# A hybrid decoder layer on one core: the opening loads cut smaller and put on two queues, with small matmuls of ones between the first products

## The chip, the cores and the metric

The kernel runs on one core of a Trainium2 chip. The metric is the device time of one execution in microseconds; where several runs were timed, the median is given. The profile is one execution taken by the hardware profiler, and its times are counted from the start of its span.

## What is computed

One layer of a decoder step, for 1,024 prompt tokens and 8 x 4 sample tokens, at a model width of 1,024, all in float32. Cut to its frame:

```python
h = rms(x, n_mix_pre)
z = h @ w_in                       # q | k | v | u, 512 + 128 + 128 + 512 columns
a = sliding_window_attention(q, k, v, sinks)
m = pool_mixer(u) @ w_pool * pool_scale
x = x + rms(concat(a, m) @ w_out, n_mix_post)
f = rms(x, n_ffn_pre)
x = x + rms((silu(f @ w_gate) * (f @ w_up)) @ w_down, n_ffn_post)
x = x + sigmoid(x @ w_ple_gate) * (p @ w_ple)
```

The change concerns the first product alone, the `u` columns of `h @ w_in`, and the loads and casts ahead of it.

## The kernel before

The 1,056 tokens are cut into three groups `g` of 352. Activations lie with their features on the 128 partitions and their tokens along the free axis, so x of one group is eight tiles of 128 x 352, held as two halves `h` of four tiles each. The text calls half `h` of group `g` x(g,h). A weight of 1,024 x 128 is eight tiles of 128 x 128, again used in two halves.

To keep float32 accuracy with float32r operands, each operand is split in two: a part `hi` (weights `wh`) that ScalarE casts to float32r, and the remainder `lo` (weights `wl`) that VectorE subtracts (`split`, L163). A product is then three matmuls per tile: `wh` with `hi`, `wh` with `lo`, `wl` with `hi`. For x the cast also multiplies by the norm's gain `gn` (`x_operand`, L359: ScalarE at L364, VectorE at L366). The norm's own factor per token is applied only afterwards, at the eviction of `u` (L476).

The opening goes like this. Constants and a table of ones are made on GpSimd; the gains are loaded over ScalarE's queue (L139, called at L142). ScalarE computes a square root once, so that its table is loaded (L343). TensorE runs 8 matmuls of ones with ones, of 128 columns in float32 (L346). SP issues all the other loads in a fixed order (`load`, L339; L392 to L402): the first half of weight 0, x(0,0) in two parts, the first halves of weights 1 to 3, x(0,1), the second halves of weights 0 and 1, x(1,0), the second halves of weights 2 and 3, x(1,1). The casts on ScalarE and the subtractions on VectorE are pinned to the order in which they are written, from L403 to L415 (`fixed`): the first half of weight 0, x(0,0), the first halves of weights 1 to 3, x(0,1), the second halves of weights 0 and 1, x(1,0), the second halves of weights 2 and 3, and then the squares of x(0,0) and x(0,1) on ScalarE (L375) and their sum over the eight tiles on VectorE (`sum_halves`, L326), which gives `acc`. What comes after on these two engines is not pinned: the tool that builds the program places it by a schedule of its own.

TensorE's matmuls are pinned throughout (`pinned`, L485). The order is: for each half, the products of weights 0 to 3 with group 0 (`u_prod`, L461: per tile `wh` with `hi` and `wh` with `lo`, then four times `wl` with `hi`); then the norm of group 0, in two steps of `rstd_steps` (L292). The first step sums `acc` over the partitions (L300), ScalarE takes the root (L302), VectorE the reciprocal (L303) and builds two diagonal matrices `dg` (L310). Between the steps TensorE does the product of weight 0 with x(1,0). The second step multiplies `dg` by ones (L320), which spreads the factor over the partitions. Then the products with groups 1 and 2, the other columns of `w_in`, attention, the output projection and the feed-forward, which fills most of the span.

Of the kernel before, what the change touches and what calls it, by code (L numbers as in the profile page):

```python
# [11 lines left out]
F32R = mybir.dt.float32r  # L12
AF = mybir.ActivationFunctionType
# [3 lines left out]
P = 128  # L17
D = 1024
KC = D // P
# [35 lines left out]
WARM = 8  # L55
# [6 lines left out]
def trunk_kernel(  # L62
# [31 lines left out]
    nc = tc.nc  # L94
    te, ve, se, ge = nc.tensor, nc.vector, nc.scalar, nc.gpsimd
# [10 lines left out]
    def nm(s):  # L106
        cnt[0] += 1
        return f"{s}{cnt[0]}"

    def act_tile(shape, dt=F32, s="a"):  # L110
        return apool.tile(shape, dt, tag="a", bufs=A_SLOTS, name=nm(s))

    def half(g, dt=F32, s="h"):
        return act_tile([P, 4, NS[g]], dt, s)
# [9 lines left out]
    def mm(*args, **kw):  # L124

        ins = te.matmul(*args, **kw)  # L126
        if pinned[0]:
            tc.keep_in_program_order(ins)

    def bank():  # L130
        return psum.tile([P, 512], F32, tag="b", name=nm("b"))
# [4 lines left out]
    def const(shape, src=None, s="c", dt=F32):  # L136
        t = cpool.tile(shape, dt, name=nm(s))
        if src is not None:
            nc.scalar.dma_start(t, src)  # L139
        return t  # L140

    gn = const([P, 4, KC], gains)  # L142
    psc, skp, skd = const([P, 4]), const([P, 8]), const([P, 2])
    ident = const([P, P])
    make_identity(nc, ident)
    ones = const([P, P])
# [3 lines left out]
    epst = const([P, 1])  # L150
# [3 lines left out]
    plan = []  # L154
# [3 lines left out]
    def fix(ins):  # L158

        if fixed[0]:  # L160
            tc.keep_in_program_order(ins)

    def split(hi, lo, src):  # L163
        fix(se.copy(hi, src))  # L164
        fix(ve.tensor_tensor(lo, src, hi.bitcast(F32), op=ALU.subtract))  # L165

    raws, pairs = {}, {}
# [9 lines left out]
    def w_tile(shape, s):  # L177
        return wpool.tile(shape, F32R, tag="wp", bufs=2 * W_PAIRS, name=nm(s))
# [45 lines left out]
    for s, gs in WALK:  # L224
        pairs_of = []
        for i in range(SLAB):
            c = SLAB * s + i
# [108 lines left out]
        return r.unsqueeze(1).to_broadcast([P, 4, r.shape[1]])  # L336


    def load(dst, src):  # L339
        tc.keep_in_program_order(nc.sync.dma_start(dst, src))  # L340


    tc.keep_in_program_order(se.activation(const([P, 1]), epst, AF.Sqrt))  # L343
    warm = bank()
    for _ in range(WARM):
        te.matmul(warm[:, :P], ones, ones, start=True, stop=True)  # L346

    xr = {}

    def x_load(g, h, n=1):  # L350
        xr[g, h] = half(g, s="xr")
        for c in range(0, 4, 4 // n):
            cs = slice(c, c + 4 // n)
            k = slice(4 * h + c, 4 * h + c + 4 // n)
            load(xr[g, h][:, cs, :], x[:, k, OFF[g] : OFF[g + 1]])

    xs, acc1, r1 = [[None] * 2 for _ in range(G)], [None] * G, [None] * G

    def x_operand(g, h):  # L359
        t = xr[g, h]  # L360
        hi, lo = half(g, F32R), half(g, F32R)
        for c in range(4):
            gc = gn[:, 0, 4 * h + c : 4 * h + c + 1]
            fix(se.activation(hi[:, c, :], t[:, c, :], AF.Identity, scale=gc))  # L364
            fix(
                ve.scalar_tensor_tensor(  # L366
                    lo[:, c, :], t[:, c, :], gc, hi[:, c, :].bitcast(F32), op0=ALU.mult, op1=ALU.subtract
                )
            )
        xs[g][h] = hi, lo  # L370

    def x_squares(g):
        sqs = [xr[g, h] for h in range(2)]
# [2 lines left out]
        acc1[g] = sum_halves(sqs, g)  # L376


    def u_load(c, h):
        j = U0[c]  # L380
        if h == 0:
            shape = plan[j][1]
            raws[j] = act_tile(shape) if c == 3 else wpool.tile(shape, F32, tag="wr", bufs=W_RAW, name=nm("wr"))
        load(raws[j][:, 4 * h : 4 * h + 4, :], plan[j][0][:, 4 * h : 4 * h + 4, :])

    def u_split(c, h):
        j = U0[c]
        if h == 0:
            pairs[j] = w_tile(plan[j][1], "wh"), w_tile(plan[j][1], "wl")
        split(*(t[:, 4 * h : 4 * h + 4, :] for t in pairs[j]), raws[j][:, 4 * h : 4 * h + 4, :])  # L390

    u_load(0, 0)  # L392
    x_load(0, 0, 2)
    for c in range(1, 4):
        u_load(c, 0)
    x_load(0, 1)
    for c in range(2):
        u_load(c, 1)
    x_load(1, 0)
    for c in range(2, 4):  # L400
        u_load(c, 1)
    x_load(1, 1)  # L402
    fixed[0] = True  # L403
    u_split(0, 0)
    x_operand(0, 0)
    for c in range(1, 4):
        u_split(c, 0)
    x_operand(0, 1)
    for c in range(2):
        u_split(c, 1)  # L410
    x_load(2, 0)
    x_operand(1, 0)
    for c in range(2, 4):
        u_split(c, 1)
# [4 lines left out]
    for dst, src in ((psc, pscale), (skp, sink_p), (skd, sink_d)):  # L419
        load(dst, src)  # L420
# [12 lines left out]
    n = 4 * NDEC * PST  # L433
# [27 lines left out]
    def u_prod(c, g, h):  # L461

        if h == 0:
            ups[c, g] = bank()
        ps = ups[c, g][:, : NS[g]]
        wh, wl = pairs[U0[c]]
        xh, xl = xs[g][h]
        for k in range(4):
            mm(ps, wh[:, 4 * h + k, :], xh[:, k, :], start=h == 0 and k == 0, stop=False)
            mm(ps, wh[:, 4 * h + k, :], xl[:, k, :], start=False, stop=False)  # L470
        for k in range(4):
            mm(ps, wl[:, 4 * h + k, :], xh[:, k, :], start=False, stop=h == 1 and k == 3)

# [14 lines left out]
    for h in range(2):  # L488
        for c in range(4):
            u_prod(c, 0, h)  # L490
    u_norm(norms[0], 0)
    u_prod(0, 1, 0)
    x_operand(2, 0)
    u_norm(norms[0], 0)
    x_squares(1)
    for c in range(4):
        u_evict(c, 0)
        if c:
            u_prod(c, 1, 0)
# [79 lines left out]
    for c in range(4):  # L579
        n = NDEC * DSEQ  # L580
# [67 lines left out]
    def scores(b):  # L648


        t = act_tile([P, 8, WIN])
        cur = [bank() for _ in range(2)]
        prv = [bank() for _ in range(2)] if b else None
        for c in range(4):
            for which, at in ((cur, b), (prv, b - 1)):
                if which is None:
                    continue
                for kv in range(2):
                    rows = slice(64 * kv, 64 * kv + 64)
                    mm(  # L660
                        which[kv][:, c * WIN : (c + 1) * WIN],
                        qT[c][rows, b * WIN : (b + 1) * WIN],
                        kT[rows, at * WIN : (at + 1) * WIN],
                        start=True,
                        stop=True,
                    )
        for kv in range(2):
            tk = t[:, 4 * kv : 4 * kv + 4, :]
            if b:
                se.copy(tk, v4(prv[kv]))  # L670
                ve.copy_predicated(tk, m4(0).bitcast(mybir.dt.int32), v4(cur[kv]))  # L671
            else:
                ve.tensor_tensor(tk, v4(cur[kv]), m4(1), op=ALU.add)
            hs = slice(4 * kv, 4 * kv + 4)
            softmax(tk, 4, 0.125, skp[:, hs], nskp[:, hs])
        return t
# [145 lines left out]
    t = scores(order[0])  # L822
# [15 lines left out]
    for a, b in zip(order, order[1:] + [None]):  # L838
# [5 lines left out]
        t = t2  # L844
# [421 lines left out]
```

## Time and profile before

| | us |
|---|---|
| median of 3 runs | 1123.25 |
| lowest and highest | 1122.29, 1125.07 |
| the profiled execution | 1121.84 |
| its span | 1120.1 |
| TensorE busy in the span | 1108.9 |
| VectorE busy | 748.4 |
| ScalarE busy | 440.7 |

In the rows below, a row of the timeline has the start, the busy time, the engine, the line, the operation with its output and inputs, a count, and in brackets the idle time of that engine before it and what ended it. PE is TensorE, DVE is VectorE, ACT is ScalarE, SPq is SyncE's queue of load instructions. A row of waits has the engine and line, what it waited for, and the total, the number of times and the longest in us. A row of stretches has the stretch, its length, the busy time of PE, weight loads, DVE, ACT and POOL with their counts, then TensorE's granted clock as a share of full, the share of the DMA engines and GB/s. A row of load issues ends in the KB of one load and the us from its issue to its landing.

### The profile page before, as it was taken

The page shows a single profiled execution, that of the slowest core. Times are in us where ns is not written, and L with a number is a line of the kernel's source. Part 1 is how long each engine was busy: PE and PEld are TensorE (multiplying, and loading weights), DVE is VectorE, ACT ScalarE, POOL GpSimd, SP SyncE. Part 2 cuts the span into 40 slices and gives each one's busy share as a digit, 9 for nine tenths or more (in the row PEclk, how much of TensorE's full clock was granted, in tenths as well). Part 3 has the DMA queues.
Part 4 walks back from the last instruction along what each step waited for, and adds up shares of the span by engine and source line. Part 5 has one row for each costly group of instructions (what it writes and reads, how often), then busy time and mean ns, then how long its engine had stood idle before and what let it go on. Part 6 is the DMA issues. An engine that isn't in the chain of part 4 may idle for free.

```text
span 1120.1 us, 17702 instructions
## 1 busy us (share of the span) xinstructions
PE 1108.9 (99%) x7171; PEld 1090.8 (97%) x7171; DVE 748.4 (67%) x1244; ACT 440.7 (39%) x782; POOL 179.5 (16%) x152
## 2 busy tenths in 40 slices
PE   8999999999999999999999999999999999999998
PEld 8999988899999999999999999999999999999998
DVE  6667468985879955355554555557887877789532
ACT  8323276664646524331321314124424334366220
POOL 0045132200000041011111101111132123100000
PEclk9999999999999999999999999999999999999999
DMA  8121311272543312111110212112212222246211
GB/s 288 57 70 43 119 41 38 83 265 71 206 159 132 114 38 76 39 61 54 38 57 20 75 38 76 39 39 93 104 57 77 74 76 79 96 161 215 91 58 39
DMA packets 35265, 99.54 MB, mean 89 GB/s; under 512 B 4180, under 2 KB 14708, under 8 KB 35184
## 3 DMA queue, kind: packets, MB, share of 16 engines
q1 hardware_dynamic: 33856, 96.65, 25.6%
q10 hardware_dynamic: 1328, 1.77, 0.5%
q8 instruction: 56, 0.92, 0.4%
q14 instruction: 25, 0.20, 0.1%
HBM read 88.30 MB, written 10.11 MB: 88 GB/s over the span
## 4 chain that ended last, share of the span: by engine, by line
PE 88%; DVE 6%; ACT 3%; DMA 1%; issue 1%; POOL 0%; SPq 0%; DVEq 0%; ACTq 0%; POOLq 0%
PE b L126 88%; ACT a L634 1%; DVE wl L165 1%; DMA xr<-in_x_dram 1%; DVE mx L626 1%; DVE a L671 1%; ACT wh L164 1%; POOL wr L980 0%; DVE h L366 0%; PE b L120 0%; DMA c<-in_gains_dram 0%; DVE o L1107 0%; DVE x L1111 0%; DVE a L734 0%; DVE p L1014 0%
## 5 line engine op out<-in xcount | busy, mean ns | idle before, releaser
L126 PE MATMUL b<-fh,wh 128*128 128x352 f32 x808 | 260.7, 323 | 0.0
L126 PE MATMUL b<-fh,wl 128*128 128x352 f32 x808 | 259.3, 321 | 0.0
L126 PE MATMUL b<-fl,wh 128*128 128x352 f32 x808 | 259.0, 321 | 0.0
L126 PE MATMUL b<-hid,wh 128*128 128x352 f32 x1056 | 252.5, 322 | 1.7 <-DVE o L1107 1.2
L164 ACT CAST wh<-wr 128x1024 fp32r<-128x1024 f32 (+1 forms) x139 | 142.9, 1030 | 249.6 <-PE b L126 206.6
L165 DVE TENSOR_TENSOR wl<-wr,wh 128x1024 fp32r<-128x1024 f32 (+1 forms) x139 | 171.7, 1238 | 63.8 <-ACT wh L164 63.6
L126 PEld LDWEIGHTS b<-hid,wh 128*128 128x128 f32 x1056 | 182.3, 188 | 2.5 <-issue 1.5
L126 PE MATMUL b<-hid,wl 128*128 128x352 f32 x528 | 169.0, 320 | 0.0
L980 POOL TENSOR_TENSOR wr<-wr 128x512 f32<-128x512 f32 x44 | 63.4, 1441 | 622.3 <-DVE wl L165 451.8
L126 PEld LDWEIGHTS b<-fl,wh 128*128 128x128 f32 x808 | 151.8, 188 | 0.0
L126 PEld LDWEIGHTS b<-fh,wl 128*128 128x128 f32 x808 | 151.8, 188 | 0.0
L126 PEld LDWEIGHTS b<-fh,wh 128*128 128x128 f32 x808 | 151.6, 188 | 0.0
L1077 DVE TENSOR_TENSOR o<-o,b 128x352 f32<-128x352 f32 x240 | 114.7, 514 | 27.3 <-PE b L126 27.2
L126 PE MATMUL b<-fh,sh 128*128 128x352 f32 x352 | 113.6, 323 | 0.0
L126 PE MATMUL b<-fl,sh 128*128 128x352 f32 x352 | 112.8, 320 | 0.0
L126 PE MATMUL b<-fh,sl 128*128 128x352 f32 x352 | 112.7, 320 | 0.0
L126 PE MATMUL b<-h,wh 128*128 128x352 f32 x480 | 106.1, 327 | 1.3 <-ACT h L364 0.9
L165 DVE TENSOR_TENSOR sl<-wr,sh 128x1024 fp32r<-128x1024 f32 x44 | 53.7, 1222 | 75.5 <-ACT sh L164 75.5
L126 PEld LDWEIGHTS b<-hid,wl 128*128 128x128 f32 x528 | 99.0, 187 | 0.0
L164 ACT CAST sh<-wr 128x1024 fp32r<-128x1024 f32 x44 | 45.7, 1047 | 130.9 <-POOL wr L980 91.3
L126 PEld LDWEIGHTS b<-h,wh 128*128 128x128 f32 x480 | 82.6, 190 | 2.6 <-DVE h L366 1.3
L126 PE MATMUL b<-h,wl 128*128 128x352 f32 x240 | 66.3, 325 | 0.0
(150 smaller groups left out, 1593.3 us busy)
## 6 DMA issues: line engine op xcount, KB each, us to landing
wr<-in_w_gu_dram SPq DMA_DIRECT2D x64, 512.0 KB, 3.3
wr<-in_w_dn_dram SPq DMA_DIRECT2D x32, 512.0 KB, 3.5
wr<-in_w_pg_dram SPq DMA_DIRECT2D x14, 512.0 KB, 3.7
x<-in_x_dram SPq DMA_DIRECT2D x6, 704.0 KB, 7.7
x1d<-x SPq DMA_DIRECT2D x6, 704.0 KB, 3.5
x<-x1d SPq DMA_DIRECT2D x6, 704.0 KB, 6.2
out_y_dram<-yo SPq DMA_DIRECT2D x24, 176.0 KB, 1.8
wr<-in_w_out_b_dram SPq DMA_DIRECT2D x8, 512.0 KB, 3.3
```

Of the source, the lines that this page charges most:

```text
L126: ins = te.matmul(*args, **kw)
L164: fix(se.copy(hi, src))
L165: fix(ve.tensor_tensor(lo, src, hi.bitcast(F32), op=ALU.subtract))
L626: ve.tensor_reduce(mx, t, axis=AX.X, op=ALU.max)
L634: se.activation(t[:, c, :], t[:, c, :], AF.Exp, bias=nmx[:, c : c + 1], scale=scale, accum_out=sm[:, c : c + 1])
L671: ve.copy_predicated(tk, m4(0).bitcast(mybir.dt.int32), v4(cur[kv]))
L980: ge.tensor_tensor(out, a, b, op=op)
L1077: ve.tensor_tensor(o, o, v, op=ALU.add)
```

## The change

The first half of weight 0 is loaded in two parts of two tiles, the first over ScalarE's queue and the second over SP's; x(0,0) is loaded in four parts instead of two; the gains follow the first part of the weight on ScalarE's queue. The casts of these parts are pinned in the order x tile 0, weight tiles 0 and 1, x tile 1, weight tiles 2 and 3, x tiles 2 and 3. In the first product (weight 0, group 0, half 0), after each tile's two matmuls, comes one matmul of ones with ones, of 64 columns in float32, into the PSUM bank that the opening's ones matmuls used. The square root and the opening's ones matmuls stand after the two loads on ScalarE's queue. Cut to its core:

```diff
-    gn = const([P, 4, KC], gains)
+    gn = const([P, 4, KC])
...
+    u_load(0, 0, (0, 1), nc.scalar)
+    load(gn, gains, nc.scalar)
...
     tc.keep_in_program_order(se.activation(const([P, 1]), epst, AF.Sqrt))
     warm = bank()
     for _ in range(WARM):
         te.matmul(warm[:, :P], ones, ones, start=True, stop=True)
...
-    u_load(0, 0)
-    x_load(0, 0, 2)
+    x_load(0, 0, 4, range(2))
+    u_load(0, 0, (2, 3))
+    x_load(0, 0, 4, range(2, 4))
     for c in range(1, 4):
         u_load(c, 0)
...
     fixed[0] = True
-    u_split(0, 0)
-    x_operand(0, 0)
+    x_operand(0, 0, range(1))
+    u_split(0, 0, (0, 1))
+    x_operand(0, 0, range(1, 2))
+    u_split(0, 0, (2, 3))
+    x_operand(0, 0, range(2, 4))
     for c in range(1, 4):
         u_split(c, 0)
...
             mm(ps, wh[:, 4 * h + k, :], xh[:, k, :], start=h == 0 and k == 0, stop=False)
             mm(ps, wh[:, 4 * h + k, :], xl[:, k, :], start=False, stop=False)
+            if (c, g, h) == (0, 0, 0):
+                mm(warm[:, :64], ones, ones[:, :64], start=True, stop=True)
```

The helpers `x_load`, `x_operand`, `u_load` and `u_split` take the tiles to act on as a further argument, and `load` the queue; nothing else in them differs.

More of the change, by code (lines that the diff above doesn't have):

```diff
@@ L336, in bc4, with load, x_load @@
         return r.unsqueeze(1).to_broadcast([P, 4, r.shape[1]])
[L339 to L346, printed above, removed]
+    def load(dst, src, q=nc.sync):
+        tc.keep_in_program_order(q.dma_start(dst, src))
     xr = {}
-    def x_load(g, h, n=1):
-        xr[g, h] = half(g, s="xr")
-        for c in range(0, 4, 4 // n):
+    def x_load(g, h, n=1, cs=range(4)):
+        if (g, h) not in xr:
+            xr[g, h] = half(g, s="xr")
+        for c in cs[:: 4 // n]:
             cs = slice(c, c + 4 // n)
@@ L357, in trunk_kernel, with x_operand @@
     xs, acc1, r1 = [[None] * 2 for _ in range(G)], [None] * G, [None] * G
-    def x_operand(g, h):
+    def x_operand(g, h, cs=range(4)):
         t = xr[g, h]
-        hi, lo = half(g, F32R), half(g, F32R)
-        for c in range(4):
+        if xs[g][h] is None:
+            xs[g][h] = half(g, F32R), half(g, F32R)
+        hi, lo = xs[g][h]
+        for c in cs:
             gc = gn[:, 0, 4 * h + c : 4 * h + c + 1]
@@ L369, in x_operand @@
             )
-        xs[g][h] = hi, lo
     def x_squares(g):
@@ L376, in x_squares, with u_load, u_split @@
         acc1[g] = sum_halves(sqs, g)
-    def u_load(c, h):
+    def u_load(c, h, k=range(4), q=nc.sync):
         j = U0[c]
-        if h == 0:
+        ks = slice(4 * h + k[0], 4 * h + k[-1] + 1)
+        if j not in raws:
             shape = plan[j][1]
             raws[j] = act_tile(shape) if c == 3 else wpool.tile(shape, F32, tag="wr", bufs=W_RAW, name=nm("wr"))
-        load(raws[j][:, 4 * h : 4 * h + 4, :], plan[j][0][:, 4 * h : 4 * h + 4, :])
-    def u_split(c, h):
+        load(raws[j][:, ks, :], plan[j][0][:, ks, :], q)
+    def u_split(c, h, k=range(4)):
         j = U0[c]
-        if h == 0:
+        ks = slice(4 * h + k[0], 4 * h + k[-1] + 1)
+        if j not in pairs:
             pairs[j] = w_tile(plan[j][1], "wh"), w_tile(plan[j][1], "wl")
-        split(*(t[:, 4 * h : 4 * h + 4, :] for t in pairs[j]), raws[j][:, 4 * h : 4 * h + 4, :])
-    u_load(0, 0)
-    x_load(0, 0, 2)
+        split(*(t[:, ks, :] for t in pairs[j]), raws[j][:, ks, :])
+    u_load(0, 0, (0, 1), nc.scalar)
+    load(gn, gains, nc.scalar)
+    tc.keep_in_program_order(se.activation(const([P, 1]), epst, AF.Sqrt))
+    warm = bank()
+    for _ in range(WARM):
+        te.matmul(warm[:, :P], ones, ones, start=True, stop=True)
+    x_load(0, 0, 4, range(2))
+    u_load(0, 0, (2, 3))
+    x_load(0, 0, 4, range(2, 4))
     for c in range(1, 4):
```

## The prediction

> **What bounds the kernel now.** I read the page's first part, then TensorE's waits, then the first 30 us engine by engine. All times are us from the span's start.
>
> ```profile
> PE 1108.9 (99%) x7171; PEld 1090.8 (97%) x7171; DVE 748.4 (67%) x1244; ACT 440.7 (39%) x782; POOL 179.5 (16%) x152
> ```
>
> ```profile
> PE b L126 <- DVE o L1107: 1.2, 1, 1.2
> ...
> PE b L126 <- DVE dg L310: 0.8, 2, 0.4
> ```
>
> TensorE is busy for 99% of the span, and its longest single wait is 1.2 us, far behind the change. So whatever the change does happens in the opening: once TensorE runs without a break, the rest follows it. The question is where the opening's time goes. The granted clock by stretch:
>
> ```profile
> 4.90:8.40 3.50, 2.18 (x9) 1.28 (x9) 2.78 (x6) 2.95 (x6) 0.00 (x0) 1.00 1.02 343
> 8.40:11.80 3.40, 3.40 (x12) 3.40 (x13) 2.34 (x5) 2.08 (x5) 0.00 (x0) 0.50 1.01 355
> 11.80:15.20 3.40, 3.40 (x23) 3.40 (x22) 3.17 (x7) 2.96 (x7) 0.00 (x0) 1.00 1.06 394
> ```
>
> After 3.5 us in which TensorE was busy for only 2.18, one stretch of 3.4 us ran at half clock (0.50). Half of it is a loss to TensorE: 1.7 us. The instructions on TensorE:
>
> ```profile
> 1.12 3.79 PE L346 MATMUL b<-c 128*128 128x128 f32 x16 [1.12 <-POOL c L147]
> 5.84 0.42 PE L126 MATMUL b<-h,wh 128*128 128x352 f32 x1 [0.94 <-ACT h L364]
> ...
> 8.69 1.38 PE L126 MATMUL b<-h,wl 128*128 128x352 f32 x4
> 9.86 2.33 PE L126 MATMUL b<-h,wh 128*128 128x352 f32 x8
> ...
> 12.67 1.44 PE L126 MATMUL b<-h,wh 128*128 128x352 f32 x8
> ...
> 14.59 1.44 PE L126 MATMUL b<-h,wh 128*128 128x352 f32 x8
> ...
> 24.22 0.71 PE L126 MATMUL b<-c,acc 128*88 128x1 f32 x8
> 24.80 1.53 PE L126 MATMUL b<-h,wh 128*128 128x352 f32 x8
> ...
> 27.36 0.77 PE L126 MATMUL b<-dg,c 88*128 88x352 f32 x2 [0.39 <-DVE dg L310]
> ```
>
> One product of twelve matmuls took 12.67 - 9.86 = 2.81 us, mostly at half clock, and 14.59 - 12.67 = 1.92 at full clock: 0.16 a matmul. Eight such products (96 matmuls) end at 24.22, where the norm's sums (the eight records with `acc`) begin; then a ninth; then at 27.36 TensorE waits for `dg`. The row that matters most is not TensorE's. These are ScalarE and VectorE:
>
> ```profile
> 7.49 1.12 ACT L164 CAST wh<-wr 128x512 fp32r<-128x512 f32 x2
> 8.53 0.62 ACT L164 CAST wh<-a 128x512 fp32r<-128x512 f32 x1
> 10.47 2.03 ACT L364 ACTIVATE h<-xr,c 128x352 fp32r<-128x352 f32 x4 [1.31 <-DMA xr<-in_x_dram]
> ...
> 13.96 2.03 ACT L364 ACTIVATE h<-xr,c 128x352 fp32r<-128x352 f32 x4 [0.44 <-DMA xr<-in_x_dram]
> ...
> 16.93 1.38 ACT L375 ACTIVATE xr<-xr 128x1408 f32<-128x1408 f32 x1
> ...
> 23.33 1.36 ACT L375 ACTIVATE xr<-xr 128x1408 f32<-128x1408 f32 x1
> 24.97 0.26 ACT L302 ACTIVATE sd<-b,c 88x4 f32<-88x4 f32 x1 [0.29 <-PE b L126]
> ```
>
> ```profile
> 19.61 1.62 DVE L329 TENSOR_TENSOR xr<-xr,xr 128x1408 f32<-128x1408 f32 x1 [1.74 <-ACT xr L375]
> ...
> 22.95 0.51 DVE L332 TENSOR_TENSOR acc<-xr 128x352 f32<-128x352 f32 x1
> 23.38 2.56 DVE L366 SCALAR_TENSOR_TENSOR h<-xr,c,h 128x352 fp32r<-128x352 f32 x5
> 25.86 0.17 DVE L303 RECIPROCAL sd<-sd 88x4 f32<-88x4 f32 x1
> 25.95 0.55 DVE L366 SCALAR_TENSOR_TENSOR h<-xr,c,h 128x352 fp32r<-128x352 f32 x1
> ...
> 26.70 0.95 DVE L310 TENSOR_TENSOR dg<-c,hl 88x352 fp32r<-88x352 f32 x2
> ```
>
> From 13.96 on ScalarE works without a gap until its squares are done, and VectorE without one from 19.61 to `dg`. What starts them is a load; the chain that ended last says the same:
>
> ```profile
> 5.40 8.54 DMA xr<-in_x_dram
> ...
> 27.36 42.69 PE b L126 x270
> ```
>
> x(1,0), the first half of the second token group, is issued at 5.40 and lands at 13.94. From there 13.4 us of ScalarE and VectorE work lead to 27.36, where TensorE starts a run of 42.69 us without a wait. The eight products run beside this chain: TensorE comes to the sums 0.76 us after `acc` is ready (24.22 against 22.95 + 0.51 = 23.46), and to `dg` 0.39 us too early. That is all the chain leaves it.
>
> **The change part by part.**
>
> *Order of the first casts and the smaller loads.* The first activation of x now goes ahead of the cast of half of w. Before, the first product started at 5.84. Now a 128 KB part of w goes by ScalarE's queue while x starts on SP's. How early these land, the issue rows bound:
>
> ```profile
> c<-in_gains_dram ACTq DMA_DIRECT2D x1, 16.0 KB, 3.4
> wr<-in_w_in_dram SPq DMA_DIRECT2D x1, 256.0 KB, 3.3
> ```
>
> 16 KB took as long as 256 KB, so half the bytes may land no sooner: at most some tenths are won. The gains are now second on ScalarE's queue, so they are issued one issue (about 0.4) later than 0.71 and land near 4.5; the first activation needs them. Activation (2.03 / 4 = 0.51) and a half cast (at most a whole one, 1.12 / 2 = 0.56) end near 5.5: the first product gains 0.3 us (bounds 0 and 0.8). The last of the four x parts is cast near 7.5 as before, since ScalarE does the same work; the extra cast and the extra VectorE subtraction (under 0.56 each) lie in the waits there, and behind them in ScalarE's 1.31 before 10.47; without that cover they would cost 0.56. The table load on ScalarE starts two issues later, still in its idle time before 4.00.
>
> The Trainium skill, page "DMA: Bandwidth & Descriptors", section "Issuing engines are not separate DMA queues", says that a second issuing engine saves only the sequencer's time to start a transfer. By it the second queue alone would bring one issue, about 0.4 us, at the very start; the two rows above, which show a fixed part of about 3.3 us, do not speak against it.
>
> *SP's queue.* Three more loads are issued in all, two of them net on SP ahead of everything else. Each takes about 0.45 us of SP, so x(0,1) and x(1,0), the issues quoted next, come about 0.9 us later. SP also waits there for earlier loads to land (second fence), and in the new order x(1,0) would stand behind a part of x that landed at 6.5 before: 1.1 later. I take 1.0.
>
> ```profile
> 3.60 0.43 SPq L340 DMA_DIRECT2D xr<-in_x_dram  x1
> ...
> 5.40 0.58 SPq L340 DMA_DIRECT2D xr<-in_x_dram  x1
> ```
>
> ```profile
> SPq L340 <- DMA xr<-in_x_dram: 0.5, 1, 0.5
> ```
>
> ```profile
> 0.00:5.00 5.00, 3.79 (x16) 3.49 (x16) 0.35 (x1) 2.10 (x3) 1.28 (x13) 1.00 0.60 182
> 5.00:10.00 5.00, 3.77 (x13) 2.88 (x14) 4.28 (x8) 3.70 (x7) 0.00 (x0) 0.84 1.03 357
> ```
>
> By 5.40 the engines had moved 5.0 x 182 + 0.4 x 357 = 1,050 KB of the 3,015 KB issued ahead of x(1,0) (six half weights of 262 and two halves of x of 721). So nearly 2 MB stand in line, over five us of work at 357 GB/s; a load issued 1 us later lands when the bytes ahead of it are through, not later. And the bytes are the same. Bounds of the shift of x(1,0)'s landing: 1.0 us later if the issue decides, and earlier by
>
> ```profile
> 2.00:3.00 1.00, 1.00 (x7) 1.00 (x7) 0.00 (x0) 0.64 (x2) 0.00 (x0) 1.00 0.97 246
> 3.00:4.00 1.00, 1.00 (x6) 1.00 (x6) 0.00 (x0) 0.00 (x1) 0.00 (x0) 1.00 0.86 270
> ```
>
> (357 - 246) + (357 - 270) = 198 KB, or 0.55 us, if two queues fill these two microseconds to the full rate. I take half of that, 0.3 us earlier, since the bytes in line speak against the late end and the share of 0.97 against the whole early one.
>
> *Ones between the first products.* Four matmuls of 64 columns are eight records on TensorE. The nearest rows are the 16 of 128 columns (3.79 / 16 = 0.24 each) and the eight of one column (24.80 - 24.22 = 0.58, 0.07 each): 0.6 to 1.9 us, and I take 0.8. From 5.84 to 8.69 TensorE had eight matmuls of 0.16 to do, 1.3 of 2.85 us; the waits for the x parts cover 0.8, with at most one ones matmul (0.2) left bare. What they may bring: the stretch to 8.4 is then busier, and the clock may stay full, which gives TensorE the 1.7 us back.
>
> The Trainium skill, page "TensorE: Matmul & The Clock Gate", section "HAM oscillation — how this bites in real kernels", asks only that no idle gap exceed about 3.4 us. Here the clock fell with no wait over 0.94 us in the stretch, so the measurement decides: it is the share of work that counts. By that rule the ones would change nothing and the clock would have stayed up anyway.
>
> *The sum.* TensorE's own path to 24.22: -0.3 (start) - 1.7 (clock) + 0.2 (ones) = -1.8, so 22.4. But `acc` is ready only at 23.46 - 0.3: it waits 0.8 there. The ninth product then ends near 25.9, and `dg` comes from VectorE, busy without a gap since 19.61, at 27.36 - 0.3: it waits again, 1.1 us where it was 0.39. So 1.5 of the 1.8 us are swallowed by two waits, and 0.3 us is left. Behind 27.36 it passes through: TensorE has no wait in the next 42.69 us. The profiled execution took 1121.84 (span 1120.1 and 1.74 around it), 1.41 under the median; 1121.84 - 0.3 = 1121.5, on the median's scale 1122.9.
>
> **The rivals.**
>
> *The reciprocal moves up.* VectorE's order behind the pinned part is set when the program is built. The reciprocal stands behind five L366, though its input was there at 25.23 (24.97 + 0.26). With the sums starting at 23.3, the square root is bound by the square at 23.33 (done 24.69) and the reciprocal could run at 25.0 instead of 25.86 if the program places it ahead of one or two of them; with 0.3 from the loads: -1.2 us, 1122.0. For it: TensorE's part is early enough. Against it: the order need not change.
>
> *The ones do not hold the clock.* If 8 matmuls and 8 short records are still too little in that stretch, half clock stays. TensorE reaches the sums at 24.0, and the end is the loads' alone: -0.2, 1123.0.
>
> *The loads come later* (the other side). If x(0,1) and x(1,0) land as much later as they are issued, ScalarE's 13.96 becomes 15.0, everything to 27.36 moves with it: +1.0, 1124.3. It decides as soon as x(1,0) lands after 13.94, as ScalarE has only 0.44 us of slack that this very load made.
>
> *The clock falls later instead.* TensorE now waits 0.8, does light sums for 0.6 and waits 1 us more between 22.4 and 27: a stretch of 3.4 us about as empty as the one before 8.4. Half clock in the next one costs 1.7, less 0.3: 1124.7. The skill's page on the clock gate calls its window free-running; no single trace can show that, and it would make this differ by execution.
>
> **How the numbers follow.** Forecast 0.45, reciprocal 0.22, no hold 0.15, late loads 0.10, clock later 0.08. The range takes the late loads' end and most of the clock's, on the fast side the reciprocal's with 1 us for what the runs differ among themselves (1122.29 to 1125.07): 1121.0 to 1124.9. No case reaches 0.3% (3.4 us, about what a measurement of this kernel can tell from no change). TensorE's whole excess in the opening is 27.36 - 5.84 - 9 x 1.92 - 0.58 = 3.7 us, so faster by 3.4 would need nearly all of it: 0.03. Slower by 3.4 would need both last rivals and more: 0.04. Same: 0.93.
>
> **What would show it.** Right: full clock from 8.4 on, twelve matmuls in 1.92 us by the second product, TensorE at the sums near 22.4 to 23.2 with a wait for VectorE's `acc` (L332), then a wait near 1 us for `dg` in place of 0.39, and the unbroken run from about 27.1. Wrong: x(1,0) activated well off 13.7 (before 13 or after 14.4); a reciprocal at 25.3 or earlier; a 0.50 stretch at another place; or a difference that arises behind 60 us, where the argument has none.

## The result, and the profile after

The changed kernel is slower by a small amount that is clear of noise: a median of 1126.89 us (1124.41 to 1128.73, 13 runs) against 1122.63 us (1122.00 to 1125.07, 13 runs) for the kernel before, run beside it. The ratio is 1.003, 95% interval 1.002 to 1.004, so some 4 us of loss where 0.3 us of gain was forecast. The profiled execution took 1126.98 us, with a span of 1125.2 us: 5.1 us more than that of before.

The changed opening, first as SP and ScalarE issue it. A row of the timeline of SP (SPq) or of ScalarE's queue (ACTq) is one or more loads issued back to back:

```profile
0.72 0.86 SPq L340 DMA_DIRECT2D xr<-in_x_dram  x2
1.63 0.42 SPq L340 DMA_DIRECT2D wr<-in_w_in_dram  x1
2.10 0.91 SPq L340 DMA_DIRECT2D xr<-in_x_dram  x2
3.05 1.61 SPq L340 DMA_DIRECT2D wr<-in_w_in_dram  x2
4.71 0.43 SPq L340 DMA_DIRECT2D a<-in_w_in_dram  x1
5.18 0.44 SPq L340 DMA_DIRECT2D xr<-in_x_dram  x1
...
6.69 0.69 SPq L340 DMA_DIRECT2D xr<-in_x_dram  x1
```

```profile
0.71 0.41 ACTq L340 DMA_DIRECT2D wr<-in_w_in_dram  x1
1.16 0.45 ACTq L340 DMA_DIRECT2D c<-in_gains_dram  x1
...
5.03 0.59 ACT L361 ACTIVATE h<-xr,c 128x352 fp32r<-128x352 f32 x1 [1.89 <-DMA c<-in_gains_dram]
...
15.83 2.03 ACT L361 ACTIVATE h<-xr,c 128x352 fp32r<-128x352 f32 x4 [0.46 <-DMA xr<-in_x_dram]
```

The pair of weight loads at 3.05 took SP 1.61 us where a pair took 0.94 before: the second of them waited. x(0,1) was issued at 5.18 (3.60 before), x(1,0) at 6.69 (5.40 before), and x(1,0) was activated at 15.83 instead of 13.96. The gains, now second on ScalarE's queue, held the first activation until 5.03. The chain that ended last names the same loads:

```profile
0.71 3.60 DMA wr<-in_w_in_dram
4.32 0.02 issue
4.33 0.33 SPq L340
...
6.69 9.11 DMA xr<-in_x_dram
...
25.38 4.71 PE b L126 x22
```

SP's wait ended when the very first load, the weight part on ScalarE's queue, had landed at 4.32. What the DMA engines and TensorE's clock did, in stretches (the last three columns are the clock, the DMA share and GB/s):

```profile
7.00:8.00 1.00, 0.96 (x6) 0.62 (x5) 1.00 (x4) 1.00 (x3) 0.00 (x0) 1.00 0.87 134
8.00:9.00 1.00, 1.00 (x8) 1.00 (x9) 0.99 (x2) 0.26 (x2) 0.00 (x0) 1.00 0.53 158
...
8.40:11.80 3.40, 3.40 (x24) 3.40 (x24) 1.98 (x3) 1.24 (x2) 0.00 (x0) 1.00 0.96 335
...
25.70:29.20 3.50, 3.50 (x16) 3.50 (x16) 3.47 (x11) 3.50 (x6) 1.47 (x2) 0.51 0.09 29
872.20:875.70 3.50, 3.50 (x13) 3.50 (x14) 3.50 (x8) 0.00 (x0) 0.00 (x0) 0.51 0.27 109
```

The same two microseconds of before, whose sum is 757 KB against 292 KB here:

```profile
7.00:8.00 1.00, 0.81 (x4) 0.54 (x4) 0.86 (x2) 1.00 (x3) 0.00 (x0) 1.00 1.00 363
8.00:9.00 1.00, 1.00 (x5) 0.80 (x5) 1.00 (x3) 1.00 (x3) 0.00 (x0) 0.68 1.05 394
```

465 KB were not moved in that time, 1.2 us at the rate of 394. From 8.40 to 11.80 TensorE did 24 matmuls at full clock where it did 12 before, as forecast; but half clock came back at 25.70 and at 872.20. VectorE's last step of `acc`, and TensorE:

```profile
24.80 0.52 DVE L332 TENSOR_TENSOR acc<-xr 128x352 f32<-128x352 f32 x1
```

```profile
5.96 0.76 PE L126 MATMUL b<-h,wh 128*128 128x352 f32 x2 [1.06 <-ACT wh L164]
6.56 0.33 PE L126 MATMUL b<-c 128*128 128x64 f32 x2
6.70 0.85 PE L126 MATMUL b<-h,wh 128*128 128x352 f32 x2
...
22.47 0.81 PE L126 MATMUL b<-h,wl 128*128 128x352 f32 x4
25.38 1.04 PE L126 MATMUL b<-c,acc 128*88 128x1 f32 x8 [2.10 <-DVE acc L332]
26.27 2.69 PE L126 MATMUL b<-h,wh 128*128 128x352 f32 x8
...
29.60 0.49 PE L126 MATMUL b<-dg,c 88*128 88x352 f32 x2
...
872.13 0.81 PE L126 MATMUL b<-hid,wh 128*128 128x352 f32 x2 [2.11 <-DVE o L1121]
```

TensorE was through its eight products at 23.28 (22.47 + 0.81) and waited 2.10 us for `acc`; the sums and the ninth product then took 4.2 us, nearly all at half clock, and it came to `dg` at 29.60, 2.24 us later than before. The two matmuls with `dg` took 0.49 instead of 0.77, so behind them it was 1.96 us late (30.09 against 28.13). The last row is one that serves as a milestone; it is the matmul that waits for the tile `o` late in the span, and in before it stood here:

```profile
868.51 0.56 PE L126 MATMUL b<-hid,wh 128*128 128x352 f32 x2 [1.21 <-DVE o L1107]
```

So 3.6 us of the loss were there by 872, and the half clock behind it brought the rest (5.1 at the end of the span).

### The profile page after: what moved, and what is told of

Read it like the earlier page. It is cut to its first block, busy times and chain, and to the rows that moved or that the text cites. A ratio compares the mean times of both kernels' runs of the same rounds, so it can differ in the third digit from the quotient of the medians.

```text
span 1125.2 us, 17726 instructions
## 1 busy us (share of the span) xinstructions
PE 1111.2 (99%) x7179; PEld 1093.2 (97%) x7179; DVE 748.9 (67%) x1245; ACT 440.6 (39%) x783; POOL 180.1 (16%) x152
## 4 chain that ended last, share of the span: by engine, by line
PE 88%; DVE 5%; ACT 3%; DMA 2%; issue 1%; POOL 0%; SPq 0%; DVEq 0%; ACTq 0%; POOLq 0%
PE b L126 87%; ACT a L648 1%; DVE wl L165 1%; DMA xr<-in_x_dram 1%; DVE mx L640 1%; DMA a<-in_dmask_dram 1%; DVE a L685 1%; ACT wh L164 1%; POOL wr L994 0%; DMA wr<-in_w_gu_dram 0%; DMA wr<-in_w_in_dram 0%; DVE o L1121 0%; DVE x L1125 0%; DVE a L748 0%; PE b L120 0%
## 5 line engine op out<-in xcount | busy, mean ns | idle before, releaser
L164 ACT CAST wh<-wr 128x1024 fp32r<-128x1024 f32 (+2 forms) x140 | 143.2, 1024 | 252.6 <-PE b L126 205.5
L165 DVE TENSOR_TENSOR wl<-wr,wh 128x1024 fp32r<-128x1024 f32 (+2 forms) x140 | 171.4, 1226 | 62.3 <-ACT wh L164 62.1
L126 PEld LDWEIGHTS b<-fl,sh 128*128 128x128 f32 x352 | 66.2, 188 | 0.0
```

## The experiments

Theory A: the landing of x(1,0) decides, and it is late because the small first loads use up the loads that may be under way at once, so that SP stalls; the ones change nothing that reaches the end, but may let the clock fall in the wait that they create. Rivals: B, the ones themselves or the new order of the casts cost the time; and that the fall of the clock is the cost, whatever the loads do. The ratios below are to the kernel before, run beside each (its medians were 1122.63 beside after, and 1122.51, 1122.52 and 1122.32 beside the others).

| kernel | x(1,0) activated | TensorE at `dg` | between | matmul that waits for `o` | median (low to high, runs) | ratio, 95% |
|---|---|---|---|---|---|---|
| before | 13.96 | 27.36 | 13.40 | 868.51 | 1122.3 to 1122.6 | |
| after | 15.83 | 29.60 | 13.77 | 872.13 | 1126.89 (1124.4 to 1128.7, 13) | 1.003, 1.002 to 1.004 |
| ones alone | 13.79 | 29.88 | 16.09 | 872.23 | 1128.45 (1127.4 to 1128.9, 5) | 1.0045, 1.0033 to 1.0057 |
| loads alone | 15.40 | 28.80 | 13.40 | 870.94 | 1125.26 (1124.3 to 1127.3, 11) | 1.0022, 1.0013 to 1.0030 |
| x in two parts | 14.23 | 28.28 | 14.05 | 870.64 | 1123.73 (1123.2 to 1127.0, 11) | 1.0010, 1.0002 to 1.0019 |
| ones in the wait | 15.78 | 31.88 | 16.10 | 873.34 | 1129.10 (1125.8 to 1130.4, 6) | 1.0050, 1.0037 to 1.0064 |
| norm first | none | 25.61 | | 867.35 | 1121.94 (1120.3 to 1123.3, 12) | 0.9994, 0.9985 to 1.0002 |
| norm first, ones | none | 25.52 | | 868.25 | 1122.80 (1121.5 to 1126.6, 12) | 1.0005, 0.9994 to 1.0016 |
| two parts, no ones | 15.09 | 28.52 | 13.43 | 870.24 | 1123.45 (1122.2 to 1125.2, 12) | 1.0007, 0.9999 to 1.0015 |
| gains by GpSimd | 14.85 | 28.24 | 13.39 | 870.91 | 1124.57 (1123.3 to 1126.5, 12) | 1.0018, 1.0009 to 1.0026 |
| wait filled, order kept | 15.72 | 29.10 | 13.38 | 871.33 | 1124.63 (1123.8 to 1126.5, 11) | 1.0019, 1.0010 to 1.0027 |
| ones alone, order kept | 14.06 | 27.89 | 13.83 | 869.23 | 1123.06 (1122.0 to 1125.0, 11) | 1.0004, 0.9995 to 1.0013 |
| after, order kept | 16.60 | 29.98 | 13.38 | 872.25 | 1125.95 (1124.8 to 1130.0, 6) | 1.0035, 1.0023 to 1.0048 |

The columns of times are from one profiled execution each ("none": x(1,0) is no longer in that chain). Wherever TensorE waits for `dg` and the order of the norm is unchanged, `dg` comes 13.38 to 13.43 us after x(1,0) is activated, in six kernels with landings from 13.96 to 16.60. In three more TensorE was itself the later one (13.77, 13.83, 14.05).

**Loads alone, and ones alone.** The change split in two. Loads alone is after without the ones; ones alone is before with

```diff
+            if (c, g, h) == (0, 0, 0):
+                mm(warm[:, :64], ones, ones[:, :64], start=True, stop=True)
```

> The changed kernel without the ones matmuls between the first products. Theory A: x(1,0) lands near 15.8 as in the changed kernel, TensorE goes on near 29.4 against 27.4 before, about 2 us more: 1124.7, and less of a wait for acc than the 2.1 us of the changed kernel if the half-clock stretch at 8.4 returns. Theory B: the time of before, 1122.6.

> The kernel before with the four ones matmuls alone, its loads and casts untouched. Theory A (the loads come late in the changed kernel, and the wait that follows drops the clock): here x(1,0) lands near 13.9 as before, the half-clock stretch at 8.4 disappears, TensorE comes to the sums near 22.4, waits about 1 us for acc and again for dg, and goes on at 27.4: 1122.6, within 0.7, and up to 1.7 more where the wait lets the clock fall. Theory B (the ones matmuls themselves do the harm): 1125 or more.

Loads alone kept most of the loss: 1125.26, near A's 1124.7 and clear of B's 1122.6. The 1.6 us between it and after are not clear of noise, as the intervals overlap. TensorE, less early without the ones, waited 1.07 and 1.02 us, and the clock stayed full:

```profile
24.96 0.79 PE L126 MATMUL b<-c,acc 128*88 128x1 f32 x8 [1.07 <-DVE acc L332]
...
28.80 0.78 PE L126 MATMUL b<-dg,c 88*128 88x352 f32 x2 [1.02 <-DVE dg L310]
```

Ones alone was slower still, 1128.45, and only B had asked for 1125 or more; here are its VectorE and its TensorE:

```profile
26.18 1.62 DVE L329 TENSOR_TENSOR xr<-xr,xr 128x1408 f32<-128x1408 f32 x1
27.71 0.17 DVE L303 RECIPROCAL sd<-sd 88x4 f32<-88x4 f32 x1
...
29.22 0.95 DVE L310 TENSOR_TENSOR dg<-c,hl 88x352 fp32r<-88x352 f32 x2
```

```profile
29.88 0.77 PE L126 MATMUL b<-dg,c 88*128 88x352 f32 x2 [1.65 <-DVE dg L310]
```

The four instructions made the tool that builds the program place the unpinned work otherwise: the reciprocal stands behind the 1.62 us sum of the next group's squares, and `dg` is 2.5 us later than before. Not all of that is the order, as in this profile TensorE also came to the sums 1.27 us later (25.49 against 24.22). So this kernel alone can't tell the ones from the order; the next one can. (In the kernel after, the order of VectorE and ScalarE behind the opening is that of before.)

**Ones alone, order kept.** The same ones, with the norm's instructions pinned to the order that they have in before: root, reciprocal, `dg`, the sums and the operands around them go through `fix`, in that order; one copy on ScalarE and one eviction on VectorE stand a place off.

```diff
-        ve.reciprocal(sd[:w], sd[:w])
+        fix(ve.reciprocal(sd[:w], sd[:w]))
```

> The kernel before with the four small ones matmuls alone, and the order of the norm's instructions on VectorE and ScalarE pinned to that of the kernel before. Theory A (the ones themselves neither help nor cost, as TensorE's gain is waited off at the sums and at dg, and the 6 us of the first ones-only kernel came from the order): 1122.2 to 1122.9. Theory B (the ones cost, whatever the order): 1125 or more. Theory C (the ones hold the clock and that reaches the end): 1121.0.

1123.06, not to be told from before, and 5.4 us under ones alone: B is out, and the ones show neither a help nor a cost (0.6 us of gain to 1.5 us of loss by the interval). Its TensorE:

```profile
25.31 0.71 PE L126 MATMUL b<-c,acc 128*88 128x1 f32 x8
...
27.89 0.74 PE L126 MATMUL b<-dg,c 88*128 88x352 f32 x2
```

and its stretch of the opening:

```profile
8.40:11.80 3.40, 3.40 (x14) 3.40 (x14) 2.37 (x5) 2.09 (x5) 0.00 (x0) 1.00 1.03 357
```

14 matmuls in 3.4 us are about what half clock allows (12 before, 24 after), though the clock column says 1.00: the trace's first record of the clock comes only at 12.49, and ahead of it the column reads 1.00. With ones in place, TensorE did 24 there in after and 23 in norm first with ones, but 14 to 18 in the seven other profiles with ones; without ones it was 12 to 21 in four. The ones do not fix when the clock is full.

**x in two parts.** The kernel after with x(0,0) in two loads, ones and all:

```diff
-    x_load(0, 0, 4, range(2))
+    x_load(0, 0, 2, range(2))
...
-    x_load(0, 0, 4, range(2, 4))
+    x_load(0, 0, 2, range(2, 4))
```

> The changed kernel with x(0,0) in two loads instead of four, the weight still in two. Theory A, in its form that SP may have only eight loads under way and small ones leave too few bytes in line: the ninth load is now x(0,1) and not the first half of weight 2, so the first halves of weights 1 to 3 are issued without a wait, the line does not run dry between 6.5 and 8.5 us, and x(1,0) lands between 13.9 and 14.8; 1123 to 1125. If only the number of issues on SP counts (0.45 us each): 0.9 us less than the changed kernel, 1126.0. Theory B: no change, 1126.9.

3.2 us of the loss went, with 1123.73 and x(1,0) activated at 14.23, both as A had it; the count of issues alone (1126.0) and B (1126.9) are out. The new order of the casts is in this kernel too, so it can cost no more than the 1.2 us that are left over before. SP's queue, and the stretches that had run dry:

```profile
3.17 0.45 SPq L340 DMA_DIRECT2D a<-in_w_in_dram  x1
4.68 0.38 SPq L340 DMA_DIRECT2D xr<-in_x_dram  x1
```

```profile
7.00:8.00 1.00, 1.00 (x5) 1.00 (x5) 1.00 (x4) 1.00 (x3) 0.00 (x0) 1.00 1.05 389
8.00:9.00 1.00, 1.00 (x5) 1.00 (x5) 1.00 (x3) 1.00 (x3) 0.00 (x0) 1.00 1.06 391
```

SP's stall is now two loads further on, ahead of x(0,1), and the engines stay at 389 and 391 GB/s. In after and in this kernel alike, the first load that stalls is the ninth on the two queues of SP and ScalarE together.

**Two parts, no ones.** The same without the ones.

> The run e3_x_two_parts without the ones matmuls; again the order on every other engine is the same in both. If the ones help where the loads come in time: 0.5 to 1.5 more than e3_x_two_parts (1124.2 to 1125.2). If they only cost their own time: 0.3 to 1.2 less (1122.5 to 1123.4).

1123.45 against 1123.73, with intervals that overlap: the ones again change nothing that can be measured. In this profile the first load took 4.4 us to land (3.6 in after), so the ninth was issued only at 5.11, and x(1,0) was activated at 15.09, later than the 14.8 that A allowed. With or without them the new order of the casts stays within some 1 us of before.

**Gains by GpSimd.** A test of the count of eight: after, with the gains' load on GpSimd's queue.

```diff
-    load(gn, gains, nc.scalar)
+    load(gn, gains, nc.gpsimd)
```

> The changed kernel with its gains loaded over GpSimd's queue, so one load fewer is on the two other queues, with x(0,0) still in four parts. If a limit of eight loads under way on these queues is what held SP (theory A): the first half of weight 2 is issued near 3.5 without its wait of 0.8 us, weight 3 is the one that waits (until about 4.3), x(0,1) is issued little sooner than 5.18 and the line still runs short: 0 to 1 us less than the changed kernel, 1126 to 1126.9. If it is the wait for the gains or the load on ScalarE's queue that counts: x(1,0) lands near 14 and 1124.

```profile
3.05 0.91 SPq L340 DMA_DIRECT2D wr<-in_w_in_dram  x2
4.16 0.33 SPq L340 DMA_DIRECT2D a<-in_w_in_dram  x1
4.53 0.43 SPq L340 DMA_DIRECT2D xr<-in_x_dram  x1
```

```profile
5.13 0.59 ACT L361 ACTIVATE h<-xr,c 128x352 fp32r<-128x352 f32 x1 [2.45 <-DMA c<-in_gains_dram]
```

The pair at 3.05 passes without a wait, and the next load, now the ninth, waits until 4.16, as A had it. The time did not come as A had it: all four small parts of x are still there, yet x(1,0) came a microsecond earlier and the median fell by 2.3 us, where A had asked for 0 to 1; 1124.57 is nearer the rival's 1124. But a shorter wait for the gains is not the reason, as the last row shows: the first activation still waited for them until 5.13 (5.03 in after). x(1,0) was issued only 0.14 us earlier (6.55 against 6.69); what came earlier is x(0,1), issued at 4.53 instead of 5.18, and between 7 and 9 us the engines moved 293 and 374 GB/s in place of 134 and 158.

The traces also list, for each load, the semaphore that its landing raises and the one that its issue waits for. In all thirteen kernels the opening's loads of SP and of ScalarE take the same eight semaphores in turn: the ninth load is issued only when the first has raised its own, the tenth when the second has, and so on. It is not the number under way that counts. In after the second load had landed at 4.14, so that at most seven were under way, and the ninth still waited for the first, until 4.32. The kernel's text contains no such wait, so it comes from the tool that builds the program; the load on GpSimd's queue raises a semaphore outside the eight. So the limit that these runs show is one of the program, and none of them shows one of the chip.

**Ones in the wait, and wait filled with the order kept.** Does the clock fall because TensorE waits 2.1 us? Eight ones matmuls ahead of the sums of after:

```diff
+    for _ in range(8):
+        mm(warm[:, :P], ones, ones, start=True, stop=True)
     u_norm(norms[0], 0)
```

> The changed kernel with eight more ones matmuls of 128 columns ahead of the norm's sums, where TensorE waited 2.1 us for acc. Theory A: TensorE goes on near 29.5 less what the half clock took after the sums; the stretch of half clock that began at 25.4 is gone: 1125.2, 1.7 less than the changed kernel. If that wait is not what drops the clock: 1126.9 or a little more.

The clock did not fall, but the median was 1129.10, above both forecasts, and the order had changed as in ones alone:

```profile
31.88 0.77 PE L126 MATMUL b<-dg,c 88*128 88x352 f32 x2 [3.00 <-DVE dg L310]
```

So it was made again with the order of after pinned, beside a control that has the pins and not the filler:

> The kernel after, with eight ones matmuls of 128 columns ahead of the norm's sums as before, and now the order of the norm's instructions on VectorE and ScalarE pinned to that of the kernel after. Theory A (TensorE's wait of 2.1 us for the sums lets the clock fall, and the fall costs 1.7 us): the ones take some 1.9 of the 2.1 us, the clock is full from the sums to 32 us, dg comes where it came, and the time is 1.0 to 1.7 us under that of the same kernel without the ones: 1125.2 to 1125.9. Theory B (the fall at 25.75 was chance, or has another cause): no gain, 1126.9.

> The kernel after with the order of the norm's instructions on VectorE and ScalarE pinned to what it was; one copy on ScalarE comes one place later. A control for the kernel with the stall filled. Theory A and B: 1126.9, as the kernel after, with a wait of about 2 us for the sums. If the pinning itself changes the time, another figure.

```profile
24.38 1.95 PE L126 MATMUL b<-c 128*128 128x128 f32 x16
...
26.74 1.53 PE L126 MATMUL b<-h,wh 128*128 128x352 f32 x8
...
29.10 0.77 PE L126 MATMUL b<-dg,c 88*128 88x352 f32 x2 [0.20 <-DVE dg L314]
```

The filler takes the wait's place, and the ninth product runs at full clock. The median is 1.3 us under the control's, the size that A gave, though the intervals overlap. But the traces do not carry that: both kernels stand 13.38 us behind x(1,0) at `dg`, and the control's clock did not fall there either, since TensorE came later and waited 1.04 us, not the 2 that had been expected. x(1,0) landed 0.9 us later in the control's profile. What the fall at 25.70 costs is read from after itself: 13.77 - 13.40, some 0.4 us at `dg`, as nearly all of it lies beside the wait for `dg`; behind the two matmuls with `dg` only 0.1 is left (1.96 against the 1.87 by which x(1,0) was late). Nor does such a wait bring the fall by itself: ones in the wait stood 3.00 us at `dg`, x in two parts 1.90 and gains by GpSimd 1.88 at `o`, all at a clock that stayed full. So what makes the clock fall stays open.

**Norm first, without and with ones.** If x(1,0) bounds the chain, the norm of group 0 need not wait for it. Before's loads; the squares of group 0 ahead of x(1,0)'s operands, and the norm pinned ahead of the remainders of x(1,1):

```diff
     for c in range(2):
         u_split(c, 1)
+    x_squares(0)
     x_load(2, 0)
-    x_operand(1, 0)
     for c in range(2, 4):
         u_split(c, 1)
-    x_squares(0)
+    x_operand(1, 0)
```

> The kernel before with its loads as they were and without ones between the products, but with group 0's squares ahead of the second half of weights 2 and 3 and of x(1,0) on ScalarE, their sums likewise on VectorE, and the norm's root, reciprocal and dg pinned ahead of the lo parts of x(1,1). If the chain from x(1,0)'s landing to dg is what holds TensorE to 27.36 (theory A), it no longer does: acc is ready near 19.5, dg near 25.5, TensorE goes on at 26 to 26.5 with the clock falling at 8.4 and 1 us sooner without: 1121.5. If TensorE's own products or the loads of the weights hold it: 1122.5.

> The run e5_norm_first with the four ones matmuls added; the order on every other engine is the same in both, so the difference is that of the ones alone. If they keep the clock up from 8.4 on: 1.7 us less TensorE time, about 1 of it visible, 1120.5. If they do not, or if the stretch falls otherwise in most executions: 0 to 0.8 more than e5_norm_first.

TensorE came to `dg` at 25.61, 1.75 us earlier, with no wait at the sums or there. That is more than the 26 to 26.5 forecast, and 1.2 us of it are the clock's: it was full earlier in this profile, without ones (21 matmuls from 8.4 to 11.8 where before did 12), so TensorE was at the sums at 23.02 instead of 24.22. 1.16 us of the lead were left at 868 (867.35), and 0.1 at the end of the span (1120.0). The median of 1121.94, 0.6 under before's, can't be told from it. With ones the figure at `dg` is 25.52 and the median 1122.80, which is 0.9 more and not the gain that was hoped for. Norm first has the lowest median of all versions, and no gain is shown for it.

## Why the prediction was wrong

**The bound** was right: x(1,0)'s landing, then 13.4 us of ScalarE and VectorE, then TensorE without a wait. The table shows it in six kernels.

**SP's queue** is the step that failed: "nearly 2 MB stand in line", and so "a load issued 1 us later lands when the bytes ahead of it are through, not later". The issue of x(1,0) moved by 1.29 us (forecast 1.0), and x(1,0) came 1.87 us later, not 0.3 earlier. The 2 MB in line were counted with before's issue times. In the new order the loads ahead came later too. By 7 us the engines had moved 1,518 KB in after, about all of the 1,524 KB of its first nine loads; before had moved 1,545 KB, half of the 3,015 KB issued ahead of x(1,0). Then the rate fell to 134 and 158 GB/s where 363 and 394 had been. Why the loads issued from 4.71 on did not fill the engines sooner no run shows (in the first of these two microseconds packets still took a share of 0.87). Where the line stayed full, the step held: in ones alone, order kept, x(1,0) was issued 0.64 us later than before and activated 0.10 later (issued at 6.04, activated at 14.06).

Theory A's reason, eight loads under way, was right in the count and not in the kind: it is the ninth load that is held, but by the landing of the first. The row of a wait of SP for x was in the prediction, as a delay of 1.1 us for one load; that such a wait, met by an earlier load, can drain the engines was not weighed. So the rival "the loads come later" had the direction, and its price, 1.0, was half of what it cost at `dg`. It had a chance of 0.10. The rival of the reciprocal did not come about: its place in VectorE's order did not change.

The Trainium skill, page "DMA: Bandwidth & Descriptors", section "Issuing engines are not separate DMA queues", says that loads of several engines run on the same DMA engines; no run here tests that. Here ScalarE's queue shared one more thing with SP's, the eight semaphores; the load of 16 KB that went to GpSimd's queue took 2.3 us off the median.

**The first casts.** The first product started at 5.96, 0.12 later and not 0.3 earlier: the gains came at 5.03 and not near 4.5. The last cast of x(0,0) ended at 7.66, as forecast.

**The ones** took 0.14 us of TensorE each (6.70 - 6.56), 0.6 in all, against 0.8. In this execution the clock stayed full from 8.4 to 25.7, TensorE was at the sums at 23.28 (forecast 22.4), and the gain was waited off, as the sum had it; the wait was 2.10 and not 0.8 because `acc` was ready at 25.32 (24.80 + 0.52), 1.9 later than before and not 0.3 earlier. That the clock was full is partly luck: most other profiles with ones did not have it there.

**The clock that falls later** happened too, in the 3.4 us behind that wait, and cost 0.4 at `dg` and not the 1.7 of the rival: the wait of about 1 us for `dg` that the sum had named swallowed the rest. The second half clock, behind the 2.11 us wait for `o`, had no such cover. The Trainium skill, page "TensorE: Matmul & The Clock Gate", section "HAM oscillation — how this bites in real kernels", asks for a gap of more than about 3.4 us; both falls came behind waits of 2.1 us, so here the measurement decides. Its section "What's actually happening" has a window of 3413 ns that runs on its own; that would fit, as the half-clock stretches here are 3.4 us long and begin at different points (8.4 in before, 25.7 and 872.2 in after), and as a wait of 3.00 us passed without one.

**"Behind 27.36 it passes through"** was wrong by some tenths, and in the profiled execution by more. One more load came late in the attention of after, and one in its feed-forward:

```profile
134.29 2.68 DVE L748 TENSOR_TENSOR a<-b,a 128x512 f32<-128x512 f32 x6 [1.72 <-DMA a<-in_dmask_dram]
```

```profile
859.93 1.05 ACT L164 CAST wh<-wr 128x1024 fp32r<-128x1024 f32 x1 [1.40 <-DMA wr<-in_w_gu_dram]
```

Loads alone stands 1.44 us behind before at `dg` and 2.43 at `o`. Matmul by matmul, the distance is 1.45 until 130 us, 1.87 at 135, 2.24 at 150, and 2.43 from 210 to the end. In after it is 1.94 until 130 us, 2.15 at 135, 2.52 at 150 and 2.71 ahead of 860. The first of the three steps falls on the first of these rows, a wait that seven of the eight kernels with the new loads show (1.7 to 2.1 us). The eighth, after with the order kept, has neither that wait nor that step, but the two others. Of the five with before's loads, ones alone and norm first show the wait and the other three do not. Why the steps come was not tried.

The second row is a weight that ScalarE waited for: it makes the wait for `o` 2.11 instead of 1.21, with the half clock behind it. It came in some profiles of other kernels also (ones alone, x in two parts, gains by GpSimd) and not in loads alone or before. So the loss of after is about 2.4 us of later loads, which loads alone shows with nothing else in the way (its profiled execution took 1124.27 against 1121.84), and in about half of the runs some 2 us more (seven lie at 1126.89 or above, six at 1125.97 or below). The profiled run, at 1126.98, shows such a part at 860 to 876; that the other six have the same is not shown. Whether the change makes that second part more frequent stays open.

## What to carry to other kernels

Count the loads, not only the bytes: in this program's opening each load waits for the landing of the one eight places ahead, so cutting the first loads smaller can hold up the big ones behind them, and the queue that looks idle may share that count. Before a tuned opening gets more TensorE work or an earlier clock, see which chain the next wait ends on; here 13.4 us behind one landing decided. And look at the instruction order after any added instruction: four small matmuls on TensorE put a reciprocal on VectorE behind a sum of 1.62 us, and with the old order pinned the same kernel ran in 1123.06 us instead of 1128.45.

## What the hardware showed that was not expected

In some executions TensorE runs slightly slower for a long stretch with no wait and a full clock in the records. From 890 to 990 us, before (first) and ones alone with its order kept (second):

```profile
890.00:990.00 100.00, 100.00 (x632) 100.00 (x631) 74.70 (x117) 40.17 (x54) 22.14 (x16) 1.00 0.28 93
```

```profile
890.00:990.00 100.00, 100.00 (x623) 100.00 (x622) 73.44 (x115) 37.78 (x52) 22.25 (x16) 1.00 0.29 94
```

9 matmuls fewer at 0.16 us are 1.4 us lost, for no cause that the trace shows. Four of the thirteen profiles have it (622 to 627 matmuls, against 631 or 632 in the others), norm first among them with 627; it is most of why a lead of 1.2 us at 868 did not reach the end there, and it is as large as what half of these experiments were to tell apart.
